# Two-layer diffusion block on one core: input-projection tiles in two pools by chunk parity, attention buffers in pools of their own, halves of the scratch tensors apart, joined stores and outputs, padded addresses

## The chip, the core and the metric

The kernel runs on one core of one Trainium2 chip. The metric is the device time of one execution in microseconds. The core has a matrix engine (TensorE, PE in the profile, whose weight loads are listed as PEld), a vector engine (VectorE, DVE), a scalar engine (ScalarE, ACT), a general engine (GpSimd, POOL) and SyncE (SP), which here only issues DMAs. Data is worked on in SBUF and PSUM and moved to and from DRAM by 16 DMA engines.

## What is computed

The reference is a block of two layers over 2048 latent tokens (a grid of 32 rows by 64 columns) with a prefix of 256 context tokens, all in float32, width 1024:

```
for l in range(DEPTH):                     # 2 layers
    mod, mod_c = silu(c) @ w_mod[l] + b_mod[l], silu(c_ctx) @ w_mod[l] + b_mod[l]
    h, hc = modulate(ln_plain(x), sh1, sc1), modulate(ln_plain(ctx), csh1, csc1)
    qa, ka, va, bx, bb, bc, qn, kn, vn = split(h @ w_in[l])          # and the same of hc
    o_a = windowed_gqa_latent(rope(qa), rope(ka), va, ka_c, va_c, attn_sink[l])
    o_b = gated_short_conv(bx, bb, bc, conv_w[l])
    o_c = neighbourhood_attention_latent(qn, kn, vn, kn_c, vn_c, na_rpb[l])
    mix = concatenate([o_a, o_b, o_c]) @ w_out[l]
    x_mid = ln_affine(DEEPNORM_ALPHA * x + g1 * mix, ln1_g[l], ln1_b[l])
    ...                                    # the context tokens, in layer 0 only
    ffn = expert_choice_ffn(modulate(ln_plain(x_mid), sh2, sc2), w_router[l], w_gate[l], w_up[l], w_down[l])
    x = ln_affine(DEEPNORM_ALPHA * x_mid + g2 * ffn, ln2_g[l], ln2_b[l])
```

Head group A has 6 query heads over 2 key heads, a window of 128 tokens to either side, all context keys and a sink; group C has 6 heads, each query sees 8 grid rows by 16 columns with a bias by relative position, and all context keys.

## The kernel before

A float32 product is made of three matmuls: each operand is split into a high part (ACT's cast) and the low rest (DVE's subtraction), and high x high, low x high and high x low are added in PSUM. Names ending in `h` and `l` are these parts. PE, DVE, ACT, POOL and SP each run their instructions in the order written.

Each layer has four phases. `phase_in` (layer 0: up to about 621 us, layer 1: 2150 to 2714) normalizes the tokens, transposes them into `hh` and `hl`, and multiplies by w_in in five chunks of four 128-token tiles, the last with two. The matmuls are L627 to L629 (columns of C and B) and L805 to L807 (columns of A and V). The parts of queries and keys go to scratch tensors in DRAM: QA and KA for group A, QC and KC for group C. Each is indexed by head, then by part (high or low), then by 64 rows of the head's dimension. SBUF holds two heads over 128 partitions, so each store is cut into two DMAs of 64 partitions (loops over `b` in L659 to L661 and L785 to L788).

`phase_att` (about 621 to 1068, and 2714 to 3120) works through a list of units: A with `u` = 0, 1 (one key head and its three query heads each), and C with `u` = 0 to 5. An A unit has a block for each 128 queries; a C unit has blocks n = 0 to 3 (and n = 4, the context queries, first, in layer 0). A block goes through QK (L1061, L1062), the addition of a mask or bias with the running minimum (L1083, DVE), the exponential (L1091, ACT), transposes (L1108, L1131), copies into `ph` and `pl` (L1220 ACT, L1211 DVE), PV (L1166), a transpose back (L1179), and the division by the sum of the exponentials, which ends in a multiply on DVE (L1191). The result goes to MIXA or MIXC.

Loads are issued by SP in program order. `more_queries` keeps the queries `q` four blocks ahead, `more_values` the values `vw` of C three blocks. The key tile `k` of the next unit (high part on partitions 0 to 63, low on 64 to 127) is loaded by `load_unit`, called in the fifth block of an A unit and the second of a C unit; with it come `vx` and `toep`, from which POOL builds the next unit's bias (L1025) in two buffers, `va` and `bias`. A `k` load reads 128 rows of 2304 numbers, 1152 KB; the first of a layer comes in two parts of 320 and 832 KB, with `maskA` between. DMAs of SP take eight semaphores in turn, so each waits for the one issued eight before it.

`phase_out` multiplies by w_out (L1317) and `phase_moe` runs the 16 experts: gate and up are L1828 to L1830, down is L1865 to L1867.

Of the kernel before, what the change touches and what calls it, by code (L numbers as in the profile page):

```python
# [7 lines left out]
F32 = mybir.dt.float32  # L8
F32R = mybir.dt.float32r
# [3 lines left out]
ALU = mybir.AluOpType  # L13
# [211 lines left out]
def build(ctx, tc, t, out):  # L225
# [4 lines left out]
    const = ctx.enter_context(tc.tile_pool(name="const", bufs=1))  # L230
    dram = ctx.enter_context(tc.tile_pool(name="dram", bufs=1, space=DRAM))
# [10 lines left out]
    half = const.tile([128, 2], F32, name="half")  # L242
# [9 lines left out]
    slotc = const.tile([128, 2], F32, name="slotc")  # L252
# [128 lines left out]
    def mod_piece(l, j, ps, sb, split=True, big="gem", nbig=4, small="tr", apart=False, room=None):  # L381

        pm = ps.tile([128, 512], F32, name=big, bufs=nbig)
# [121 lines left out]
    def phase_in(l):  # L505
        es = ExitStack()
        xp = es.enter_context(tc.tile_pool(name="in_x", bufs=2))
        hp = es.enter_context(tc.tile_pool(name="hT", bufs=2))
        sb = es.enter_context(tc.tile_pool(name="in_sb", bufs=2))
        last = l == DEPTH - 1  # L510

        hT = {-1: [hp.tile([128, KD, 512], F32R, name=z) for z in ("hh", "hl")]}
# [4 lines left out]
        def prep(c):  # L517

            ts = chunk_tiles(c)
            hT[c] = [hp.tile([128, KD, 512], F32R, name=z) for z in ("hh", "hl")]  # L520
# [89 lines left out]
        ps = es.enter_context(tc.tile_pool(name="in_ps", bufs=2, space=PSUM))  # L610
        u = one.tile([128, 2, 516], F32, name="u")
# [3 lines left out]
        def gemm(c):  # L615
# [6 lines left out]
            def s_piece(key, t0=0):  # L622
                wh, wl = W.next(key)
                pg = ps.tile([128, 512], F32, name="gem", bufs=4)
# [7 lines left out]
            def c_rest(f, pg):  # L632
# [106 lines left out]
            def ctx_rest(f, pg):  # L739
# [7 lines left out]
                for a, z in enumerate((sh, sl)):  # L747
                    for b in range(2):
                        SY.dma_start((QA[l][2 * f + b] if f < 3 else KA[l][b])[a, :, 0:256], z.bitcast(F32)[64 * b:64 * b + 64])

            def a_rest(i, pg):
# [32 lines left out]
                for a, o in enumerate((qh, ql)):  # L784
                    for b in range(2):  # L785
                        z = o.bitcast(F32)[64 * b:64 * b + 64]
                        SY.dma_start(QA[l][b::2, a, :, tk].rearrange("f p n -> p f n"), z[:, 0:3, :])
                        SY.dma_start(KA[l][b, a, :, tk], z[:, 3, :])  # L788

            for kind in "AV":  # L790
# [7 lines left out]
                def one_tile(j):  # L798
                    wait_for(c, j)
                    pg = ps.tile([128, 512], F32, name="gem", bufs=4)  # L800
# [9 lines left out]
                def ctx_tiles(f):  # L810
# [3 lines left out]
                    pg = ps.tile([128, 512], F32, name="gem", bufs=4)  # L814
# [45 lines left out]
        if l == 0:  # L860
            for j in range(8):
                next(mod_piece(0, FIRST[j], ps, mb, j % 2 == 1))
                T.tick()
# [13 lines left out]
        for c in range(5):  # L877
            if l == 0 and c == 4:
                T.add(late_constants())
            for what in gemm(c):  # L880
                if what == "mod":
# [3 lines left out]
                    if mods and mods[0][0] == c:  # L885
                        next(mod_piece(0, mods.pop(0)[1], ps, mb))
# [9 lines left out]
    def phase_att(l):  # L896
        es = ExitStack()

        kp = es.enter_context(tc.tile_pool(name="at_k", bufs=2))
        qp = es.enter_context(tc.tile_pool(name="at_q", bufs=1))  # L900
        vwp = es.enter_context(tc.tile_pool(name="at_vw", bufs=3))
        op = es.enter_context(tc.tile_pool(name="at_o", bufs=6))
        mp = es.enter_context(tc.tile_pool(name="at_m", bufs=1))
        vp = es.enter_context(tc.tile_pool(name="at_v", bufs=2))
        sm = es.enter_context(tc.tile_pool(name="at_s", bufs=4))
        pp = es.enter_context(tc.tile_pool(name="at_p", bufs=3))
        hp = es.enter_context(tc.tile_pool(name="at_h", bufs=2))
        wp = es.enter_context(tc.tile_pool(name="at_w", bufs=2))
        bp = es.enter_context(tc.tile_pool(name="at_b", bufs=1))
        psl = es.enter_context(tc.tile_pool(name="at_l", bufs=2, space=PSUM))  # L910
        pst = es.enter_context(tc.tile_pool(name="at_t", bufs=3, space=PSUM))
        pso = es.enter_context(tc.tile_pool(name="at_po", bufs=1, space=PSUM))
# [5 lines left out]
        biases = [None, bp.tile([128, BWID], F32, name="bias")]  # L918
# [11 lines left out]
        NM = len(mem)  # L930
        ulist = [("A", u) for u in range(2)] + [("C", u) for u in range(6)]
# [7 lines left out]
        def load_unit(kind, u):  # L939
            r = units[kind, u] = {}  # L940
            src = (KA if kind == "A" else KC)[l][u].rearrange("a d n -> (a d) n")
            k = r["k"] = kp.tile([128, TT], F32R, name="k")
            vs = VS[l].rearrange("(i p) h d -> p i h d", p=128)
            first = loaded[0] == 0
            if kind == "A":
                r["v"] = v = vp.tile([128, NT, 128], F32R, name="va")
# [9 lines left out]
            if kind == "C":  # L956
                v = vp.tile([128, 2, 128], F32R, name="vx")
# [3 lines left out]
                tz = bp.tile([128, 16, 64], F32, name="toep", bufs=2)  # L961
# [6 lines left out]
        def load_queries(at):  # L968
# [4 lines left out]
            for x, a, y in ((0, 0, 0), (0, 1, 0), (1, 0, 1)):  # L973
                dst = q.bitcast(F32)[64 * a:64 * a + 64, x]
                if kind == "A":
                    SY.dma_start(dst[:, 0:3], QA[l][3 * u:3 * u + 3, y, :, 128 * n:128 * n + 128].rearrange("m d n -> d m n"))
                    continue
# [1006 lines left out]
```

## Time and profile before

| what | before |
|---|---|
| time, median of 3 runs | 4121.46 us (4118.05 to 4125.27) |
| profiled execution, its own time | 4118.59 us |
| its span, first to last instruction | 4116.8 us |
| mean granted TensorE clock | 0.960 of full speed |
| PE busy | 92 % of the span |
| DVE busy | 70 % |
| ACT busy | 49 % |
| POOL busy | 17 % |

The profile is of one execution. Engine shares are means over phases with different limits. SP has no busy share, since issuing a DMA is not counted as work; its timeline shows how long each issue took, with the wait in front of it where it has one. PE's busy time holds the whole length of each matmul, though the next one starts before the last has ended; how fast PE goes is read from the starts. Lines such as L951 are lines of the kernel before.

### The profile page before, as it was taken

Reading aid. Unit: us, or ns where it says so; the run is one execution under the profiler, and the core shown is the slowest. Engines: PE = TensorE matmul, PEld = TensorE weight load, DVE = VectorE, ACT = ScalarE, POOL = GpSimd, SP = SyncE. Lnnn points to the kernel's source line nnn. Section 1 sums busy time; section 2 is a strip of 40 time slices with the busy share of each in tenths; the row PEclk is TensorE's granted clock in tenths of the full one; section 3 lists DMA queues with packets and bytes.
Section 4 is the critical chain, followed back from the end, with each engine's and each line's share of the span. In section 5 each row is a group of like instructions: output and inputs, shape, how many; then the busy total and the mean of one; then the engine's idle time right before and its main releaser. Section 6 shows DMA issues by size and latency. Waiting matters only on the chain. (4 is left out here: it accounts for less than half of the span.)

```text
span 4116.8 us, 64178 instructions
## 1 busy us (share of the span) xinstructions
PE 3801.8 (92%) x22980; PEld 3241.1 (79%) x22980; DVE 2899.2 (70%) x5836; ACT 2007.7 (49%) x3918; POOL 706.6 (17%) x658
## 2 busy tenths in 40 slices
PE   7999999999898899999996999989998966999983
PEld 5877788888787378989985888888897855999972
DVE  6555558999677467767756766469996776777765
ACT  4344337988433044444434434359884332444453
POOL 0000000022123023233311000000221221222214
PEclk9999999999999999999998999999999977999996
DMA  7566665377643677777757766563676424888875
GB/s 227 172 201 206 191 191 143 94 177 175 216 162 122 201 246 219 218 217 216 209 164 225 228 196 188 171 166 107 149 177 225 162 105 153 243 248 255 248 240 184
DMA packets 768951, 785.81 MB, mean 191 GB/s; under 512 B 144912, under 2 KB 650520, under 8 KB 766584
## 3 DMA queue, kind: packets, MB, share of 16 engines
q1 hardware_dynamic: 732776, 657.53, 53.3%
q0 software_dynamic: 34704, 123.13, 10.8%
q8 instruction: 182, 2.98, 0.3%
q14 instruction: 137, 1.12, 0.1%
q10 hardware_dynamic: 1152, 1.05, 0.1%
HBM read 603.05 MB, written 178.48 MB: 190 GB/s over the span
## 5 line engine op out<-in xcount | busy, mean ns | idle before, releaser
L178 ACT CAST wh<-wraw 128x1024 fp32r<-128x1024 f32 x636 | 657.9, 1051 | 387.5 <-DMA wraw<-in_w_in 116.5
L186 DVE TENSOR_TENSOR wl<-wraw,wh 128x1024 fp32r<-128x1024 f32 x636 | 751.2, 1216 | 19.2 <-ACT wh L178 18.8
L1211 DVE TENSOR_TENSOR pl<-pt,ph 128x256 fp32r<-128x256 f32 (+2 forms) x792 | 360.7, 495 | 13.0 <-ACT ph L1220 7.9
L627 PE MATMUL gem<-hh,wh 128*128 128x512 f32 (+1 forms) x960 | 354.5, 369 | 0.0
L628 PE MATMUL gem<-hl,wh 128*128 128x512 f32 (+1 forms) x960 | 352.2, 367 | 0.0
L1091 ACT ACTIVATE p<-lg,mx 128x640 f32<-128x640 f32 (+3 forms) x408 | 332.0, 814 | 37.7 <-DVE mx L1083 36.4
L629 PE MATMUL gem<-hh,wl 128*128 128x512 f32 (+1 forms) x960 | 350.4, 365 | 0.0
L1220 ACT CAST ph<-pt 128x256 fp32r<-128x256 f32 (+2 forms) x792 | 309.5, 446 | 59.1 <-PE pt L1108 53.3
L1828 PE MATMUL pu<-xh,wh 128*128 128x288 f32 (+1 forms) x1024 | 304.6, 297 | 10.1 <-DVE sa L1656 10.1
L1828 PE MATMUL pa<-xh,wh 128*128 128x288 f32 (+1 forms) x1024 | 300.9, 294 | 0.9 <-DVE modc L419 0.9
L1061 PE MATMUL lg<-k,q 128*128 128x384 f32 (+2 forms) x768 | 280.1, 387 | 20.9 <-DMA maskA<-in_maskA 7.4
L1830 PE MATMUL pa<-xh,wl 128*128 128x288 f32 (+1 forms) x1024 | 296.9, 290 | 0.8 <-DVE wl L186 0.8
L1830 PE MATMUL pu<-xh,wl 128*128 128x288 f32 (+1 forms) x1024 | 296.4, 289 | 0.0
L1829 PE MATMUL pa<-xl,wh 128*128 128x288 f32 (+1 forms) x1024 | 294.4, 288 | 0.0
L1829 PE MATMUL pu<-xl,wh 128*128 128x288 f32 (+1 forms) x1024 | 294.1, 287 | 0.0
L1567 POOL DMA_INDIRECT xe<-H,ix x80 | 164.7, 2059 | 473.3 <-DVE ix L1562 398.2
L1062 PE MATMUL lg<-k,q 128*128 128x256 f32 x816 | 228.3, 286 | 0.4 <-ACT p L1091 0.4
L1690 POOL DMA_INDIRECT ACC<-y,ix x62 | 127.1, 2050 | 583.6 <-DVE y L1671 324.3
L1865 PE MATMUL py<-wh,gh 128*128 128x512 f32 x512 | 206.5, 403 | 17.3 <-ACT gh L1658 10.1
L805 PE MATMUL gem<-wh,hh 128*128 128x512 f32 x544 | 220.7, 406 | 0.0
L806 PE MATMUL gem<-wl,hh 128*128 128x512 f32 x544 | 217.3, 399 | 1.4 <-DVE wl L186 1.4
L807 PE MATMUL gem<-wh,hl 128*128 128x512 f32 x544 | 216.9, 399 | 0.0
(346 smaller groups left out, 9681.5 us busy)
## 6 DMA issues: line engine op xcount, KB each, us to landing
wraw<-in_w_in SPq DMA_DIRECT2D x160, 512.0 KB
wraw<-in_w_gate SPq DMA_DIRECT2D x128, 512.0 KB
wraw<-in_w_up SPq DMA_DIRECT2D x128, 512.0 KB
wraw<-in_w_down SPq DMA_DIRECT2D x128, 512.0 KB
wraw<-in_w_mod SPq DMA_DIRECT2D x88, 512.0 KB
vw<-VS SPq DMA_DIRECT2D x192, 128.0 KB
q<-QA SPq DMA_DIRECT2D x204, 96.0 KB
VS<-vs SPq DMA_DIRECT2D x36, 512.0 KB
```

What stands on the lines that cost most here:

```text
L178: self.nc.scalar.copy(h, self.raw[i])
L186: self.nc.vector.tensor_tensor(e[1], self.raw[i], e[0].bitcast(F32), op=ALU.subtract)
L627: P.matmul(pg[:, t0:nt], wh[:, cs_], hh[:, k, t0:nt], start=(k == 0), stop=False)
L628: P.matmul(pg[:, t0:nt], wh[:, cs_], hl[:, k, t0:nt], start=False, stop=False)
L629: P.matmul(pg[:, t0:nt], wl[:, cs_], hh[:, k, t0:nt], start=False, stop=(k == KD - 1))
L1061: P.matmul(pl[:, w0:512], q[:, x, m, :], win(k), start=(x == 0), stop=(x == 1))
L1091: S.activation(p[:, 0:768 - w0], rec["lg"][:, w0:768], AF.Exp, bias=st[b]["mx"][:, m:m + 1], scale=-1.0, accum_out=st[b]["ss"][:, m:m + 1])
L1211: V.tensor_tensor(view(st[b]["pl"]), src, view(st[b]["ph"].bitcast(F32)), op=ALU.subtract)
L1220: S.copy(view(st[b]["ph"]), src)
L1828: P.matmul(pp[f], wh[:, cs_], xh[:, kk, :], start=(kk == 0), stop=False)
L1829: P.matmul(pp[f], wh[:, cs_], xl[:, kk, :], start=False, stop=False)
L1830: P.matmul(pp[f], wl[:, cs_], xh[:, kk, :], start=False, stop=(kk == KD - 1))
```

## The change

- **Scratch layout.** QA, QC and KC change from head, part, row to part, head, row; KA keeps its shape but is indexed by part first. Two heads of one part then lie behind each other, and the two stores of 64 partitions become one of 128. The two parts of one head, which a `k` load reads, now lie apart: the source is taken as two times 64 rows.
- **Pools.** `hh` and `hl` get a pool for odd and one for even chunks, and the projection's PSUM tiles one of their own. Attention's pools are split and put in another order, so that the first `q`, `k`, `maskA` and `va` lie where the last chunk's `hh` and `hl` do not.
- **Joined outputs.** The sums and outputs of up to four A blocks, or two C blocks, are kept together; the small DVE and ACT instructions behind the exponentials and the last multiply run once for such a group. In A units this multiply moves from DVE to POOL, and a group has one MIXA store. The MIXC stores stay as many.
- **Addresses.** `shift` pads and the new pools move where tiles begin in SBUF. The starts of moving and stationary operands of the 512-column matmuls at L627 to L629, L805 to L807, L1317 and L1865 to L1867 all come to lie 32 bytes past a multiple of 64; before, for the stationary ones (L1317, layer 1's L1865 to L1867) or one of the two (the projection), they lay at a multiple of 64. Layer 0's L1865 to L1867 had 32 in both already.

The core of the diff:

```
+    def shift(es, n):
+        pool = es.enter_context(tc.tile_pool(name="shift", bufs=1))
+        pool.tile([128, n // 4], F32, name="shift")
...
-    QA = dr("QA", [6, 2, 64, TT])
+    QA = dr("QA", [2, 6, 64, TT])
     KA = dr("KA", [2, 2, 64, TT])
-    QC = dr("QC", [6, 2, 64, TT])
-    KC = dr("KC", [6, 2, 64, TT])
+    QC = dr("QC", [2, 6, 64, TT])
+    KC = dr("KC", [2, 6, 64, TT])
...
-        hp = es.enter_context(tc.tile_pool(name="hT", bufs=2))
+        hodd = es.enter_context(tc.tile_pool(name="hodd", bufs=1))
+        heven = es.enter_context(tc.tile_pool(name="heven", bufs=1))
...
-                    for b in range(2):
-                        SY.dma_start(dst[2 * (f % 3) + b, a, :, tok + t0:tok + nt],
-                                     z.bitcast(F32)[64 * b:64 * b + 64, t0:nt])
+                    SY.dma_start(dst[a, 2 * (f % 3):2 * (f % 3) + 2, :, tok + t0:tok + nt], z.bitcast(F32)[:, t0:nt])
...
-                    for b in range(2):
-                        z = o.bitcast(F32)[64 * b:64 * b + 64]
-                        SY.dma_start(QA[l][b::2, a, :, tk].rearrange("f p n -> p f n"), z[:, 0:3, :])
-                        SY.dma_start(KA[l][b, a, :, tk], z[:, 3, :])
+                    SY.dma_start(QA[l][a, :, :, tk].rearrange("(f b) p n -> (b p) f n", b=2), o.bitcast(F32)[:, 0:3, :])
+                    SY.dma_start(KA[l][a, :, :, tk], o.bitcast(F32)[:, 3, :])
...
-            src = (KA if kind == "A" else KC)[l][u].rearrange("a d n -> (a d) n")
-            k = r["k"] = kp.tile([128, TT], F32R, name="k")
+            src = (KA if kind == "A" else KC)[l][:, u]
+            k = r["k"] = kp[ulist.index((kind, u)) % 2].tile([128, TT], F32R, name="k")
...
-                SY.dma_start(k.bitcast(F32)[:, 128 * t0:128 * t1], src[:, 128 * t0:128 * t1])
+                SY.dma_start(k.bitcast(F32)[:, 128 * t0:128 * t1], src[:, :, 128 * t0:128 * t1])
...
+            if end:
+                V.reciprocal(of["rs"], of["ss"])
...
-            V.tensor_tensor(o[:, :nm, :], o[:, :nm, :], rec["rs"][:, :nm, None].to_broadcast([128, nm, 64]), op=ALU.mult)
+            (G if kind == "A" else V).tensor_tensor(all_, all_, of["rs"][:, :, None].to_broadcast([128, ng * nm, 64]),
+                                                       op=ALU.mult)
...
+        if last:
+            shift(es, 32)
         sb = es.enter_context(tc.tile_pool(name="moe_sb", bufs=2))
+        shift(es, 96 if last else 32)
```

PE's order does not change. On SP, the first place is the last chunk of layer 0's projection, where the queries and keys of one 128-token tile are stored from `sth` (high) and `stl` (low). Before:

```order
L787 DMA QA_81<-sth 64x3x128
L788 DMA KA_83<-sth 64x128
L787 DMA QA_81<-sth 64x3x128
L788 DMA KA_83<-sth 64x128
L787 DMA QA_81<-stl 64x3x128
L788 DMA KA_83<-stl 64x128
L787 DMA QA_81<-stl 64x3x128
L788 DMA KA_83<-stl 64x128
L736 DMA VS_89<-vs 128x1024
```

And of the change:

```order
L790 DMA QA_80<-sth 128x3x128
L791 DMA KA_82<-sth 128x128
L790 DMA QA_80<-stl 128x3x128
L791 DMA KA_82<-stl 128x128
L742 DMA VS_88<-vs 128x1024
```

Eight stores a tile become four of twice the partitions; the store of VS behind them comes four issues earlier.

The second place on SP is the fourth of the six loads of a C unit's keys in layer 1, with what each row waits for (DMAHW0 to DMAHW7 are the eight semaphores that the DMAs take in turn). Before:

```order
L951 DMA k<-KC_88 128x2304 [waits DMAHW0_49]
L958 DMA vx<-VS_90 128x2x128 [waits DMAHW1_49]
L964 DMA toep<-in_rpb 128x1x1008 [waits DMAHW2_49,Pool_49]
L1199 DMA MIXC_96<-o 8x16x64 [waits DMAHW3_49,DVE_49]
L1199 DMA MIXC_96<-o 8x16x64 [waits DMAHW4_49]
L1199 DMA MIXC_96<-o 8x16x64 [waits DMAHW5_49]
L1199 DMA MIXC_96<-o 8x16x64 [waits DMAHW6_49]
L982 DMA q_27373<-QC_86 64x8x64 [waits DMAHW7_49]
L982 DMA q_27373<-QC_86 64x8x64 [waits DMAHW0_49]
```

And of the change:

```order
L975 DMA k<-KC_87 128x1x2304 [waits DMAHW4_49]
L982 DMA vx<-VS_89 128x2x128 [waits DMAHW5_49]
L988 DMA toep<-in_rpb 128x1x1008 [waits DMAHW6_49,Pool_49]
L1006 DMA q_26886<-QC_85 64x8x64 [waits DMAHW7_49]
L1006 DMA q_26886<-QC_85 64x8x64 [waits DMAHW0_49]
L1006 DMA q_26886<-QC_85 64x8x64 [waits DMAHW1_49]
L1018 DMA vw<-VS_89 32x8x128 [waits DMAHW2_49,PE_49]
L1018 DMA vw<-VS_89 32x8x128 [waits DMAHW3_49]
L1018 DMA vw<-VS_89 32x8x128 [waits DMAHW4_49]
```

The `k` load takes the same place but has another form. The first row behind it that waits for its semaphore is, before, the second `q` (DMAHW0), eight rows on; in the change the third `vw` (DMAHW4), also eight on, since four MIXC stores have moved to where two blocks are stored together.

## Rows read from the trace of the kernel before

**Rows 1.** The page, busy time of each engine (share of the span) xinstructions.

```profile
PE 3801.8 (92%) x22980; PEld 3241.1 (79%) x22980; DVE 2899.2 (70%) x5836; ACT 2007.7 (49%) x3918; POOL 706.6 (17%) x658
```

**Rows 2.** Windows: us, then each engine's busy us (xinstructions), PEclk, DMA share, GB/s.

```profile
640.00:660.00 20.00, 20.00 (x140) 18.53 (x141) 19.61 (x59) 18.43 (x53) 0.00 (x0) 1.00 0.66 177
660.00:730.00 70.00, 69.61 (x492) 63.27 (x491) 69.11 (x222) 64.12 (x196) 0.00 (x0) 1.00 0.38 112
```

**Rows 3.** Windows, columns as above: layer 0's last projection chunk.

```profile
580.00:590.00 10.00, 4.93 (x40) 4.45 (x38) 4.15 (x10) 4.45 (x7) 0.00 (x0) 0.88 0.94 258
590.00:600.00 10.00, 9.59 (x66) 9.62 (x67) 3.23 (x6) 2.07 (x4) 1.12 (x2) 0.78 0.74 205
600.00:620.00 20.00, 20.00 (x169) 20.00 (x168) 11.53 (x24) 5.60 (x10) 0.00 (x0) 1.00 0.52 148
```

**Rows 4.** Timeline of SP in layer 1: start, us, instruction, tile, xcount.

```profile
2992.18 0.45 SPq L951 DMA_DIRECT2D k<-KC  x1
...
2996.87 6.29 SPq L982 DMA_DIRECT2D q<-QC  x3
...
3008.06 1.97 SPq L982 DMA_DIRECT2D q<-QC  x3
...
3025.75 0.46 SPq L951 DMA_DIRECT2D k<-KC  x1
```

**Rows 5.** Timeline of POOL at layer 1's last unit; brackets: idle before, releaser.

```profile
3071.25 3.23 POOL L1025 TENSOR_TENSOR bias<-maskC,toep 128x384 f32<-128x384 f32 x3 [23.89 <-DMA toep<-in_rpb]
```

**Rows 6.** Timeline of DVE at the same place.

```profile
3072.29 0.83 DVE L1083 CUSTOM_DVE_ANT_0 lg<-lg,bias 128x640 f32<-128x640 f32 x1 [0.35 <-POOL bias L1025]
```

**Rows 7.** DMA view, 2837 to 2840.6 us: packets; queue, packets, MB, share of engines.

```profile
DMA packets 448, 1.23 MB, mean 340 GB/s; under 512 B 35, under 2 KB 331, under 8 KB 335
...
q1 hardware_dynamic: 448, 1.23, 89.8%
```

**Rows 8.** DMA view of 3104 to 3112 us: busy tenths of 40 slices.

```profile
DMA  5210341000150000051033034024024005005105
```

**Rows 9.** Timeline of SP in one C unit of layer 0.

```profile
908.52 0.45 SPq L951 DMA_DIRECT2D k<-KC  x1
...
912.95 2.39 SPq L980 DMA_DIRECT2D q<-QC  x3
920.35 1.80 SPq L994 DMA_DIRECT2D vw<-VS  x4
...
946.09 0.45 SPq L951 DMA_DIRECT2D k<-KC  x1
```

**Rows 10.** Timeline of SP from the projection to attention, layer 0.

```profile
611.93 1.19 SPq L660 DMA_DIRECT2D KC<-stl  x2
621.28 1.93 SPq L976 DMA_DIRECT2D q<-QA  x3
...
633.73 0.60 SPq L951 DMA_DIRECT2D k<-KA  x1
```

**Rows 11.** Timelines of PE: layer 0's and layer 1's `down`, the projection.

```profile
1500.56 0.39 PE L1865 MATMUL py<-wh,gh 128*128 128x512 f32 x1
...
1505.59 0.39 PE L1866 MATMUL py<-wl,gh 128*128 128x512 f32 x1
...
3473.42 0.39 PE L1865 MATMUL py<-wh,gh 128*128 128x512 f32 x1
...
3478.81 0.40 PE L1867 MATMUL py<-wh,gl 128*128 128x512 f32 x1
...
134.91 0.39 PE L627 MATMUL gem<-hh,wh 128*128 128x512 f32 x1
...
142.84 0.40 PE L628 MATMUL gem<-hl,wh 128*128 128x512 f32 x1
```

**Rows 12.** Waits, 575 to 600 us: us in total, times, longest.

```profile
DVE stl L650 <- DMA KA<-stl: 6.8, 2, 4.3
```

**Rows 13.** DVE groups by shape, 660 to 730 us: busy us, mean ns.

```profile
L1191 DVE TENSOR_TENSOR o<-o,rs 128x192 f32<-128x192 f32 x14 | 5.0, 355 | 0.0
```

More of the change, by code (lines that the diff above doesn't have):

```diff
@@ L241, in build @@
     G.dma_start(ident, t["ident"])
-    half = const.tile([128, 2], F32, name="half")
+    halves = const.tile([128, 4], F32, name="half")
+    half, slotc = halves[:, 0:2], halves[:, 2:4]
     G.memset(half, -0.5)
@@ L379, in build, with mod_piece @@
     mod_done = set()
-    def mod_piece(l, j, ps, sb, split=True, big="gem", nbig=4, small="tr", apart=False, room=None):
-        pm = ps.tile([128, 512], F32, name=big, bufs=nbig)
+    def mod_piece(l, j, ps, sb, split=True, big="gem", nbig=4, small="tr", apart=False, room=None, acc=None):
+        pm = (acc or ps).tile([128, 512], F32, name=big, bufs=nbig)
         n = 4 if split else 2
@@ L861, in phase_in @@
             for j in range(8):
-                next(mod_piece(0, FIRST[j], ps, mb, j % 2 == 1))
+                next(mod_piece(0, FIRST[j], ps, mb, j % 2 == 1, acc=psg))
                 T.tick()
@@ L885, in phase_in @@
                     if mods and mods[0][0] == c:
-                        next(mod_piece(0, mods.pop(0)[1], ps, mb))
+                        next(mod_piece(0, mods.pop(0)[1], ps, mb, acc=psg))
                     continue
@@ L897, in phase_att, with pool @@
         es = ExitStack()
[L899 to L912, printed above, removed]
+        def pool(name, bufs=1, **kw):
+            return es.enter_context(tc.tile_pool(name=name, bufs=bufs, **kw))
+        qp = pool("at_q")
+        shift(es, 64)
+        kp = [pool("at_k0")]
+        mp = pool("at_m")
+        vp = [pool("at_v0")]
+        pp = pool("at_p", 3)
+        sm = pool("at_s", 3)
+        hp = [pool("at_h0")]
+        lp = [pool("at_w0")]
+        hp.append(pool("at_h1"))
+        lp.append(pool("at_w1"))
+        shift(es, 64)
+        kp.append(pool("at_k1"))
+        vp.append(pool("at_v1"))
+        op = pool("at_o", 3)
+        bsp = pool("at_bias")
+        tp = pool("at_toep", 2)
+        vwp = pool("at_vw", 3)
+        vxp = pool("at_vx", 2)
+        wp = pool("at_ot", 2)
+        bp = pool("at_b")
+        psl = [pool("at_l0", space=PSUM)]
+        pst = pool("at_t", 3, space=PSUM)
+        pso = pool("at_po", space=PSUM)
+        psl.append(pool("at_l1", space=PSUM))
         last = l == DEPTH - 1
@@ L917, in phase_att @@
         maskC = bp.tile([128, 3 * MWID], F32, name="maskC")
-        biases = [None, bp.tile([128, BWID], F32, name="bias")]
+        biases = [None, bsp.tile([128, BWID], F32, name="bias")]
         sink = sinks[:, l, :]
@@ L930, in phase_att @@
         NM = len(mem)
+        group = {}
+        for kind, u in [("A", 0), ("A", 1)] + [("C", u) for u in range(6)]:
+            for rows in (range(2, 6), range(6, 10), range(10, 14), range(14, NT), (0, 1)) if kind == "A" else (
+                    ((4,), (0, 1), (2,), (3,)) if u == 5 else ((4,), (0, 1), (2, 3))):
+                for j, n in enumerate(rows):
+                    group[kind, u, n] = ((kind, u, rows[0]), j, len(rows))
         ulist = [("A", u) for u in range(2)] + [("C", u) for u in range(6)]
@@ L1071, in soft_max @@
             if m == 0:
-                st[b] = {z: sm.tile([128, 4], F32, name=z) for z in ("mx", "ss", "rs")}
+                g, j, ng = group[b]
+                if j == 0:
+                    st["of", g] = {z: sm.tile([128, 12], F32, name=z)[:, 0:ng * nm] for z in ("mx", "ss", "rs")}
+                st[b] = {z: x[:, j * nm:j * nm + nm] for z, x in st["of", g].items()}
             first = 3e38
@@ L1180, in pv @@
             yield
[L1181 to L1184 removed]
+            if j == 0:
+                of["o"] = op.tile([128, 12, 64], F32, name="o")[:, 0:ng * nm, :]
+            all_ = of["o"]
+            o = all_[:, j * nm:j * nm + nm, :]
+            S.copy(o, px[:, :nm, 64:128])
+            if end and kind == "A":
+                V.tensor_tensor(of["ss"], of["ss"], of["rs"], op=ALU.add)
@@ L1192, in pv @@
+            n0 = g[2]
             if kind == "A":
-                SY.dma_start(MIXA[l][128 * n:128 * n + 128, 192 * u:192 * u + 192], o[:, 0:3, :].rearrange("p m d -> p (m d)"))
+                SY.dma_start(MIXA[l][128 * n0:128 * (n0 + ng), 192 * u:192 * u + 192].rearrange("(b p) c -> p b c", p=128),
+                             all_.rearrange("p (b m) d -> p b (m d)", b=ng))
             elif n == 4:
-                SY.dma_start(MIXC[l][0:256, 64 * u:64 * u + 64].rearrange("(m p) d -> p m d", p=128), o[:, 0:2, :])
+                SY.dma_start(MIXC[l][0:256, 64 * u:64 * u + 64].rearrange("(m p) d -> p m d", p=128), all_)
@@ L1196, in pv @@
             else:
                 dst = MIXC[l][256:TT, 64 * u:64 * u + 64].rearrange("(m a g b) d -> m g a b d", m=4, a=8, g=4)
-                for m in range(4):
-                    (G if b == blist[-1] else SY).dma_start(dst[m, n], o[:, m, :])
-            del st[b], blks[b]
+                for x in range(ng):
+                    for m in range(4):
+                        (G if b == blist[-1] else SY).dma_start(dst[m, n0 + x], all_[:, 4 * x + m, :])
+            del st["of", g]
         gens = []
```

57 lines of the change are left out of this document (30 added, 27 removed).

## The prediction

> **What bounds the kernel now.** I read the page first: PE is busy 92 % of the span [rows 1], so most of the kernel is bound by TensorE, and only stretches in which another engine is late, or in which each matmul gets cheaper, can give time. Then the windows, stretch by stretch. The steady A blocks of attention (660 to 730 us) show PE busy 69.61 us and DVE 69.11 us of 70: two engines are full at once, and relieving one hands the bound to the other [rows 2]. The last chunk of the layer-0 projection is the hole in the projection: 40 matmuls in 580 to 590 and 66 in 590 to 600, against 169 in the 20 us from 600 [rows 3]. Last I read SP's queue in the C units, since the change rewrites what SP loads there. In layer 1 one load of `k` comes at 2992.18 and the next at 3025.75, a unit of 33.57 us. In between SP issues almost without a gap, except that three `q` loads that took 1.97 us later took 6.29 us right behind the `k` load: 4.3 us of waiting [rows 4]. So SP, idle by the page's count, is full here. The tables of the next unit are as tight: POOL stood idle 23.89 us until `toep` landed at 3071.25, built its first piece of `bias`, and DVE had already waited 0.35 us for it at 3072.29 [rows 5, 6]. Nothing is to spare in layer 1 between landing and use.
>
> **The change, part by part.**
>
> *The `k` load.* The halves of KA and KC now lie apart in DRAM, so the source of each `k` load is two runs of 64 rows instead of 128 rows in one pattern. What does that cost? In the stretch where a 128-row load (1152 KB, 1.18 MB) makes up nearly all the traffic, the queues moved 340 GB/s with their packets on 89.8 % of 16 engines: 340 / (16 x 0.898) = 23.7 GB/s for each engine, 3.5 us for a load [rows 7]. The MIXC stores are the nearest transfers with a short outer dimension, 8 runs of 16 rows; where only they are under way (3104 to 3112), no slice shows more than 5 tenths of the engines busy [rows 8], against 89.8 % with the 128-row load. Eight outer steps reach about half of the engines. I carry that on: two outer steps reach two of 16. The load then takes 1.18 MB / 47.4 GB/s = 24.9 us. The bounds are these 24.9 us, and 3.5 us if two steps are spread as 128 rows are; I take the first, as the store of 8 steps is nearer to it in form.
>
> The Trainium skill, page "DMA: Bandwidth & Descriptors", section "Why a DMA increments its semaphore by 16 and not by 1", says that a DMA is divided over the largest number of engines, up to 16, that divides the slowest dimension larger than one of both its patterns. That gives 16 engines for the old `k` load, 8 for the MIXC store and 2 for the new load. The trace agrees for the store [rows 8]; no run here shows the two. By this rule the sum is the one below; were it wrong for two, the first rival's.
>
> Who waits: each DMA of SP waits for the one eight before it (the order of the change: `k` on DMAHW4, and the third `vw` behind it, which waits for DMAHW4). Behind it stand the later `vw`, the MIXC stores and the `q` of the next blocks. `toep` is issued two places after `k` and has its own 504 KB over 8 engines: another 64.5 KB / 23.7 = 2.7 us on the two slow engines. With 1 us from issue to start, SP is held until about 28.7 us after the issue of `k`. Before, it was free at 2996.87 + 6.29 = 3003.16, 11.0 us after [rows 4]. So 17 to 18 us are added per load; I take 17.
>
> Layer 1: no slack on SP, so the four intervals between the loads of C1 to C5 grow by 17 each, 68 us; the last load's own lateness falls on C5's first bias, which has no slack [rows 5, 6]: 17 more. 85 in all, 2 less for the slack that the first unit has. Layer 0: its interval is 946.09 - 908.52 = 37.57 us for five blocks. The wait behind `k` and `toep` is the gap from 912.95 + 2.39 = 915.34 to 920.35, and I put the small waits that remain on SP at 3 us [rows 9]. Four intervals grow by 17 - 3 = 14: 56 us. There the load is issued four blocks before its use, 4 x 37.57 / 5 = 30 us, which covers about the first lateness (15 us). 41 us. Sum for C: 83 + 41 = 124, rounded to **+125**. Bounds: 0 (spread) and 10 loads x 17 = 170. The load of C0 and that of A1 lie in the A blocks, whose SP has room; they cost nothing as long as `q` is four blocks ahead.
>
> *Attention's start.* The first `q` load waits no longer for the projection's last matmul: SP issued its last KC store at 611.93 (1.19 us) and the first `q` at 621.28 [rows 10], so loads may start 8 us earlier. But the second part of the first `k` (832 KB, 0.85 MB) takes 0.85 / 47.4 = 18.0 us on two engines: issued at 633.73 - 8, it lands at about 644, where PE was full from 640 on before [rows 2]. **+4 a layer, +8.** Bounds: -8 a layer (spread) and +12 (nothing starts earlier).
>
> *Operand addresses.* The pads and the new pools move where operands begin in SBUF. Layer 0's and layer 1's `down` matmuls (L1865 to L1867) are the same instructions at the same full clock, but in layer 0 both operands begin 32 bytes past a multiple of 64, in layer 1 the stationary one on the multiple. 22 starts in layer 0 take 1505.59 - 1500.56 = 5.03 us, 228.6 ns each; 23 in layer 1 take 3478.81 - 3473.42 = 5.39 us, 234.3 ns. The projection, whose operands differ in this remainder too, takes 142.84 - 134.91 = 7.93 us for 34, 233.2 ns [rows 11]. After the change all of these begin at 32. The compiled program has 2088 (L627 to L629), 1632 (L805 to L807), 1632 (L1317) and 768 (layer 1's `down`) such matmuls of 512 columns, 6120. At 233.2 - 228.6 = 4.6 ns: **-28 us.** Bounds: 0 (layer 1 moves more data at that time, which could be the cause instead) and 5.7 x 6120 = 35.
>
> *Joined stores.* SP's stores of QA, KA, QC and KC halve in number, with the same bytes. In the hole of rows 3, 169 - 40 - 66 = 63 matmuls are missing, 63 x 20/169 = 7.5 us, and DVE there waits up to 4.3 us for a KA store of `stl` [rows 12]. SP reaches that store four issues earlier. I take 5 of the 7.5 us, and the same in layer 1: **-10.** Bounds: 0 (bytes, not issues, are late) and 15.
>
> *Joined outputs.* In A blocks the last multiply (355 ns, 68 times in both layers [rows 13]) goes from DVE to POOL, and three small DVE instructions run once per four blocks. Up to 0.355 x 68 = 24 us of DVE leave, but PE beside it is just as full [rows 2]: **-10**, nearer to the 0 of a PE bound. In C the multiply only changes its shape. POOL's larger multiplies hide in its idle time, a few us once per four blocks; without it the MIXA store would be late, which nobody reads before the output projection. The pools by parity cost nothing in the projection: two tiles before, two after.
>
> Sum against the profiled execution's 4118.59 us: 125 + 8 - 28 - 10 - 10 = +85, 4203.6; the median lies 2.9 above that execution, so **4206 us**.
>
> **The rivals.** (1) *Two outer steps are spread over all engines, or the split costs little*: then the C term is 0 and the start gains 8 a layer: 4121.5 - 28 - 10 - 10 - 16 = 4058, faster. For it: 128 partitions are still written and a row is still 9216 bytes. Against it: rows 8. It decides from a `k` load of about 10 us downward, since 11.0 us after the issue SP is free today. (2) *Two engines, but prefetch covers most of it*: `q` is loaded four blocks ahead and `vw` three, 25 us or more. If each layer loses only about 20 us, 4121.5 + 40 + 8 - 48 = 4122, no change. Against it: the lag adds up over five loads, and in layer 1 `toep` has no slack [rows 5, 6]. (3) *The addresses do nothing*: 28 us more, 4234, with the rest as forecast.
>
> **How the numbers follow.** The forecast with its k load on two engines: 0.60 with the address gain, own range 4165 to 4235; rival 3: 0.16; rival 2, with everything from 4090 to 4150: 0.10; rival 1: 0.14. About 8 us (0.2 %) is what a measurement of this kernel tells from no change. Faster: 0.14 of rival 1 and 0.02 of rival 2; same: 0.04; slower: the rest, 0.80. The range leaves out rival 1 and the top of the C bound: 4100 to 4255.
>
> **What would show it.** Right: SP waits named `DMA k<-KC` of 15 to 20 us in every C unit, C units of about 50 us in both layers, POOL idle on `toep` some 17 us longer, PE far from full in the C windows; `down` matmuls of layer 1 at 229 ns from start to start; more than 106 matmuls in the old hole; A blocks a little shorter. Wrong: a `k` load that lands within 10 us of its issue would undo the largest term and turn the sign; a `vw` wait hidden by prefetch would shrink it.

## The result and the profile after

The changed kernel takes 4358.67 us (median of 4 runs, 4354.17 to 4360.74) against 4121.16 (4118.05 to 4125.27) of the kernel before: ratio 1.0575, 95 % interval 1.056 to 1.059. The forecast was 4206, with 4255 as the upper end. The direction was right and the size far too small, +237 us instead of +85; of the mechanism, the slow `k` load came as forecast, and part of what hangs on it did not.

To see where, I took the start of the same instruction in both traces, from stage to stage (profiled executions, spans 4116.8 and 4356.2 us, both layers together). A C unit is taken to start with DVE's addition (L1083 before) of its first block of latent queries.

| stretch | forecast | measured |
|---|---|---|
| C units, start of unit 0 to start of unit 5 | +125 | 94.2 + 105.4 = +199.6 |
| start of attention, with the second part of the first `k` | +8 | 6.8 + 6.1 = +12.9 |
| A blocks at the loads of A1's and C0's `k` | 0 | 13.1 + 9.5 + 11.5 + 10.3 = +44.4 |
| all the rest | -48 | -17.5 |
| sum | +85 | +239.4 |

The C term lies above its own upper bound of 170.

The page, busy time of each engine, beside [rows 1]:

```profile
PE 3824.4 (88%) x22980; PEld 3278.1 (75%) x22980; DVE 2870.9 (66%) x5574; ACT 2001.6 (46%) x3868; POOL 735.1 (17%) x676
```

PE falls from 92 to 88 % with the same number of matmuls: it waits more.

SP in a C unit of layer 1 answers to [rows 4]:

```profile
3117.45 0.56 SPq L975 DMA_DIRECT2D k<-KC  x1
...
3118.63 4.36 SPq L988 DMA_DIRECT2D toep<-in_rpb  x1
3123.03 20.43 SPq L1006 DMA_DIRECT2D q<-QC  x3
3143.57 4.78 SPq L1018 DMA_DIRECT2D vw<-VS  x4
3148.45 4.94 SPq L1243 DMA_DIRECT2D MIXC<-o  x8
...
3172.14 0.56 SPq L975 DMA_DIRECT2D k<-KC  x1
```

From one `k` to the next it is 54.7 us, 33.57 before. Three `q` loads, right behind `k`, take 20.43 us to issue; SP is through with them at 3143.46, 26.0 us after the `k`. What SP waits for other engines in this unit is 1.6 us in all.

POOL and DVE in the same unit, beside [rows 5, 6]:

```profile
3148.48 3.20 POOL L1049 TENSOR_TENSOR va<-maskC,toep 128x384 f32<-128x384 f32 x3 [43.47 <-DMA toep<-in_rpb]
```

```profile
3149.52 0.83 DVE L1110 CUSTOM_DVE_ANT_0 lg<-lg,va 128x640 f32<-128x640 f32 x1 [19.43 <-POOL va L1049]
```

POOL could start on `toep`, issued behind `k`, 29.9 us after its issue. POOL stood 43.47 us for it (23.89 before, in the last unit), and DVE 19.43 us for POOL (0.35 before). PE waited as well, at the first product of the next unit:

```profile
3144.32 0.66 PE L1085 MATMUL lg<-k,q 128*128 128x384 f32 x1 [14.86 <-issue]
```

The view names no releaser, but this is the first use of the `k` issued at 3117.45. A DMA adds 16 to its semaphore when it lands, in steps, and in the trace the last two steps of this `k` come at 3144.0 and 3144.2, 26.8 us after its issue. So the keys themselves were late, and the table some 4 us more.

The windows (columns as in [rows 2]); first this C unit, then the A blocks:

```profile
3117.40:3172.10 54.70, 38.40 (x269) 34.75 (x268) 33.48 (x79) 31.87 (x78) 9.57 (x9) 0.84 0.49 112
640.00:660.00 20.00, 20.00 (x144) 18.54 (x143) 18.91 (x46) 18.08 (x49) 0.00 (x0) 1.00 0.41 106
660.00:680.00 20.00, 11.71 (x84) 10.61 (x81) 12.74 (x33) 12.32 (x36) 1.47 (x1) 0.85 0.18 63
680.00:700.00 20.00, 17.55 (x107) 16.49 (x108) 13.36 (x35) 12.20 (x34) 0.85 (x1) 0.81 0.61 194
684.00:686.00 2.00, 2.00 (x9) 1.90 (x8) 1.21 (x3) 0.32 (x1) 0.00 (x0) 0.50 0.52 151
688.00:690.00 2.00, 2.00 (x16) 1.82 (x15) 1.41 (x4) 1.10 (x4) 0.00 (x0) 1.00 0.00 0
```

The unit holds 38 us of PE work in 54.7 us. In the A blocks PE, full before, is busy 11.71 us of 20 from 660 on. After the pause it first runs at the lower of its two clock levels (1.2 GHz, a granted clock of 0.50 from 684 to 686), and from 688 on at the higher one again (2.4 GHz, 1.00). With the rest of the pause this leaves 107 matmuls in the 20 us from 680, where 640 to 660 saw 144.

SP and PE's wait at this place:

```profile
649.82 0.52 SPq L975 DMA_DIRECT2D k<-KA  x1
...
653.50 27.02 SPq L1000 DMA_DIRECT2D q<-QA  x6
```

```profile
PE lg L1085 <- DMA q<-QA: 10.7, 1, 10.7
```

Behind A1's `k` six `q` loads take 27.02 us to issue, and PE runs out of queries for 10.7 us. The prediction had put this load at nothing.

In layer 0's C units the picture is another than in layer 1. The waits of SP from 880 to 1120 and of PE from 880 to 1135 hold these lines:

```profile
SPq L1018 <- DMA k<-KC: 21.1, 5, 5.1
```

```profile
PE lg L1086 <- DMA q<-QC: 41.9, 4, 11.6
PE lg L1085 <- DMA q<-QC: 14.6, 4, 4.2
```

After the hold in the issue SP still stands at a `vw` until `k` has landed, five times, each ending 27.0 to 28.7 us after the `k` was issued. PE waits there for queries, 56.5 us in eight waits, and not for the keys. Before that, in unit 0, a store is late, on SP and then on ACT:

```profile
858.72 8.13 SPq L1235 DMA_DIRECT2D MIXA<-o  x1
...
887.52 0.37 ACT L1218 COPY o<-pt 128x256 f32<-128x256 f32 x1 [20.65 <-DMA MIXA<-o]
```

It is the joined store of one group of A's last blocks, the third issue behind C1's `k` (854.17), and its last semaphore step comes at 887.4, behind the `k`'s at 882.9. ACT waits 20.65 us for its buffer of `o` (there are three), and DVE and PE stand behind ACT.

How wide is the `k` load? In 625 to 633 us the second part of layer 0's first `k` is nearly alone under way. The DMA view of that stretch, beside [rows 7, 8]:

```profile
DMA  1010101101011100100110101101011010110101
DMA packets 62, 0.41 MB, mean 52 GB/s; under 512 B 0, under 2 KB 0, under 8 KB 61
...
q1 hardware_dynamic: 61, 0.41, 12.4%
```

12.4 % of 16 engines are 2.0 engines, with 26 GB/s each. That is the forecast's step of two engines (47.4 GB/s). The Trainium skill, page "DMA: Bandwidth & Descriptors", section "Why a DMA increments its semaphore by 16 and not by 1", gives the same two, by its rule of the common divisor; the trace agrees, with 2.0.

The last projection chunk and the first loads, beside [rows 3, 10]:

```profile
580.00:590.00 10.00, 7.53 (x53) 7.29 (x54) 5.30 (x10) 4.05 (x7) 3.03 (x6) 0.83 1.11 359
590.00:600.00 10.00, 10.00 (x87) 10.00 (x87) 5.88 (x8) 4.23 (x7) 0.00 (x0) 1.00 0.67 201
```

```profile
596.65 0.33 SPq L667 DMA_DIRECT2D KC<-stl  x1
597.08 1.98 SPq L1000 DMA_DIRECT2D q<-QA  x3
...
615.50 0.54 SPq L975 DMA_DIRECT2D k<-KA  x1
```

The two slices hold 140 matmuls (106 before), in part because the whole stretch now runs some 6 us earlier. The first `q` now follows the last store at once; before there were 8 us between. From the last projection matmul to the first QK it is 7.2 us (layer 0) and 7.6 us (layer 1) less, as forecast. PE then waits for the second part of `k` until 636.90, 21.4 us after its issue:

```profile
636.90 0.66 PE L1085 MATMUL lg<-k,q 128*128 128x384 f32 x1 [12.38 <-DMA k<-KA]
```

Layer 1's `down`, beside [rows 11]:

```profile
3715.10 0.40 PE L1912 MATMUL py<-wh,gh 128*128 128x512 f32 x1
...
3720.37 0.40 PE L1914 MATMUL py<-wh,gl 128*128 128x512 f32 x1
```

23 starts in 5.27 us are 229.1 ns each (234.3 before), as forecast.

### The profile page after: what moved, and what is told of

It is laid out like the page before. It is cut to its first block, busy times and chain, and to the rows that moved or that the text cites. A ratio compares the mean times of both kernels' runs of the same rounds, so it can differ in the third digit from the quotient of the medians.

```text
span 4356.2 us, 63381 instructions
## 1 busy us (share of the span) xinstructions
PE 3824.4 (88%) x22980; PEld 3278.1 (75%) x22980; DVE 2870.9 (66%) x5574; ACT 2001.6 (46%) x3868; POOL 735.1 (17%) x676
## 5 line engine op out<-in xcount | busy, mean ns | idle before, releaser
L1085 PE MATMUL lg<-k,q 128*128 128x384 f32 (+2 forms) x768 | 291.1, 399 | 192.6 <-issue 97.2
L635 PE MATMUL gem<-hh,wh 128*128 128x512 f32 (+1 forms) x960 | 352.8, 367 | 0.0
L637 PE MATMUL gem<-hh,wl 128*128 128x512 f32 (+1 forms) x960 | 348.4, 363 | 0.0
L1085 PEld LDWEIGHTS lg<-k,q 128*128 128x128 f32 x768 | 152.5, 199 | 212.3 <-issue 167.1
L1912 PE MATMUL py<-wh,gh 128*128 128x512 f32 x512 | 206.1, 402 | 20.9 <-ACT gh L1705 12.5
L808 PE MATMUL gem<-wh,hh 128*128 128x512 f32 x544 | 220.4, 405 | 0.2 <-ACT hh L603 0.2
L1110 DVE CUSTOM_DVE_ANT_0 lg<-lg,maskA,sinks 128x640 f32<-128x640 f32 (+2 forms) x204 | 171.3, 840 | 72.1 <-PE lg L1086 71.8
```

The lines of the kernel that those rows point to most:

```text
L635: P.matmul(pg[:, t0:nt], wh[:, cs_], hh[:, k, t0:nt], start=(k == 0), stop=False)
L637: P.matmul(pg[:, t0:nt], wl[:, cs_], hh[:, k, t0:nt], start=False, stop=(k == KD - 1))
L1085: P.matmul(pl[:, w0:512], q[:, x, m, :], win(k), start=(x == 0), stop=(x == 1))
```

## The experiments

Each kernel is compared with the kernel before on the same chip. Times are medians. e1 to e4 ran on another chip than the rest; the kernel before took 4119.8 us there, and 4123.0 (e5 to e8) and 4121.4 us (e9 to e11) here, so a difference between runs of two such groups is uncertain by some 3 us. Lines of the changed kernel are kept unless the diff shows otherwise.

### Is it the `k` load? (e1, e2, e3, e4)

**e1.** The changed kernel with each `k` load as two DMAs of 64 partitions, each of which reads one run of rows.

```
-                SY.dma_start(k.bitcast(F32)[:, 128 * t0:128 * t1], src[:, :, 128 * t0:128 * t1])
+                for a in range(2):
+                    SY.dma_start(k.bitcast(F32)[64 * a:64 * a + 64, 128 * t0:128 * t1], src[a, :, 128 * t0:128 * t1])
```

> The changed kernel with each k load issued as two DMAs of 64 partitions, one for each half, so that the slowest dimension is 64 again. Theory 1 (the two-run load reaches two DMA engines and all the lost time comes from it): attention's start 7 us earlier in each layer and the cheaper projection, output projection and layer-1 down matmuls stay, the C units go back to about 37 and 33 us, so 4070 to 4095 us. Rival (the joined outputs, POOL's multiply or the new order of the pools cost a good part of the loss): still above 4150 us, with C units above 40 us.

Measured: 4119.16 us, 0.9994 [0.9984, 1.0003]. The whole +237 goes with the two-run form of the `k` load, so that form is its cause. But the 4070 to 4095 were missed: the A blocks and the rest are some 40 us better than before, and the C units lose as much again, 11.8 us in layer 0 and 26.6 in layer 1 (unit 0 to unit 5). SP in one of them:

```profile
3021.16 1.11 SPq L976 DMA_DIRECT2D k<-KC  x2
...
3029.87 7.22 SPq L1019 DMA_DIRECT2D vw<-VS  x4
3037.20 5.19 SPq L1244 DMA_DIRECT2D MIXC<-o  x8
...
3060.77 1.31 SPq L976 DMA_DIRECT2D k<-KC  x2
```

and DVE's waits in layer 1's C units (2945 to 3085 us):

```profile
DVE lg L1111 <- POOL bias L1050: 11.5, 2, 6.6
```

A unit takes 39.6 us where it took 33.6, and DVE waits for the tables. Something besides the slow load is dear in C.

**e2.** The same split for the C units alone; the A units keep the load of two runs.

```
+                if kind == "A":
+                    SY.dma_start(k.bitcast(F32)[:, 128 * t0:128 * t1], src[:, :, 128 * t0:128 * t1])
+                for a in range(2 if kind == "C" else 0):
```

> The changed kernel with the two 64-partition DMAs for the C units' k only; the A units keep the two-run load. Theory 1 splits the loss by the trace into 200 us in the C units and 57 us net in the A units and at attention's start (72 lost, 15 gained): about 4080 + 72 = 4150 us, with the A units as slow as in the changed kernel. Rival (A units are slow because of the joined outputs on POOL): the A units are slow here and in the run with both loads split, and the two runs differ by less than 20 us.

Measured: 4174.32 us, 1.0131 [1.011, 1.0151], 55 above e1. In the trace the first `k` costs 14.7 and 13.6 us more than before, A1's 12.1 and 12.0, and C0's load, split here, nothing. So the loads in the A blocks do cost, 52 us with the first ones. The 4150 were missed by 24 us, as were e1's 4095.

**e3.** The kernel before, with the scratch layout of the change and the load of two runs, nothing else (stores of 64 partitions as before).

```
-    KC = dr("KC", [6, 2, 64, TT])
+    KC = dr("KC", [2, 6, 64, TT])
...
-            src = (KA if kind == "A" else KC)[l][u].rearrange("a d n -> (a d) n")
+            src = (KA if kind == "A" else KC)[l][:, u]
```

> The kernel before with nothing changed but the scratch layout (part, head, row): stores stay at 64 partitions, the k load becomes two runs of 64 rows. Theory 1: the whole loss appears alone, without the gains: 4121 + 200 + 72 = 4390 us, within 30 us. Rival (the two-run load costs what I first worked out, 125 us, and the rest comes from joined outputs and moved MIXC stores): about 4250 us.

Measured: 4381.22 us, 1.0633 [1.0612, 1.0654]. The layout alone gives the loss, 261 us, as expected; all other parts of the change together take back some 23 us. SP of e3:

```profile
3146.80 0.56 SPq L951 DMA_DIRECT2D k<-KC  x1
...
3147.98 3.31 SPq L964 DMA_DIRECT2D toep<-in_rpb  x1
3151.39 19.93 SPq L1199 DMA_DIRECT2D MIXC<-o  x4
...
3200.89 0.56 SPq L951 DMA_DIRECT2D k<-KC  x1
```

Here the four MIXC stores stand behind `k` and `toep`, and they are held 19.93 us (2.50 in a usual block). They don't wait for their data: the multiply that made it (L1191) had ended at 3141.69. The hold falls on whatever is issued next, a store as well as a load.

**e4.** The `k` loads of C units from ACT's queue.

```
-                SY.dma_start(k.bitcast(F32)[:, 128 * t0:128 * t1], src[:, :, 128 * t0:128 * t1])
+                (S if kind == "C" else SY).dma_start(k.bitcast(F32)[:, 128 * t0:128 * t1], src[:, :, 128 * t0:128 * t1])
```

> The changed kernel with the C units' two-run k load issued from ACT's queue instead of SP's. Theory 2 (SP's next DMAs are held in their issue behind the two-run load, so most of the loss in the C units is the queue and not the late keys): the load still takes about 24 us, but SP's q, vw and MIXC go on, toep lands at once, and in layer 1 only the k load's own lateness stays, 24 - 13 = 11 us for each of five units, in layer 0 about none: 4358 - 200 + 55 = 4215 us. Rival (the two slow engines hold everything, whatever queue it is issued from): C units stay at 54 to 57 us and the time at about 4350 us.

Measured: 4409.93 us, 1.0703 [1.0681, 1.0724], slower than the change itself and outside both expectations. ACT reaches the load at 3191.72, 18.4 us after SP's `vx` at 3173.30, and SP stands all the same, in MIXC:

```profile
3182.84 34.26 SPq L1243 DMA_DIRECT2D MIXC<-o  x8
```

SP's waits from 3165 to 3222 tell for what:

```profile
SPq L1243 <- DMA k<-KC: 28.1, 1, 28.1
```

Seven of the stores go out in about 0.6 us each; the eighth waits 28.1 us for the semaphore that ACT's `k` has taken, since the DMAs of both queues take the eight semaphores in turn. SP stands so at all ten loads of C1 to C5, 286.2 us in sum. So the 4215 failed on the wait of the eighth DMA, the one that the prediction had named, and the run doesn't settle what it was made for. Only the load of C0, where SP isn't stopped so early, says something on it: in layer 0 `toep`, issued 1.6 us after ACT's `k`, took 0.68 us to issue (3.76 in the change), but a `q` load 13.1 us after that `k` took 3.21 us (usually 0.6). On another queue the hold is smaller, then, and not gone.

### What paces a C unit (e5, e6, e7, e9)

**e5.** e1, with the outputs of C blocks no longer joined (groups of one block, small pools of their own).

```
-                    ((4,), (0, 1), (2,), (3,)) if u == 5 else ((4,), (0, 1), (2, 3))):
+                    tuple((n,) for n in (4, 0, 1, 2, 3))):
```

> The kernel with the k load as two 64-partition DMAs, and the C blocks' outputs no longer joined (every C block has its own multiply and its four MIXC stores, as before the change; A stays joined). In the run with two loads the C units still lose 11 us in layer 0 and 24 us in layer 1 against the kernel before. Theory (the four MIXC stores that used to stand right behind the unit's load covered part of SP's wait for it; joined, they stand in one row of eight elsewhere): the C units return to the kernel before within 5 us a layer, 4085 to 4095 us. Rival (two 64-partition loads are themselves slower than one of 128): C units stay as in the run with two loads, about 4115 us.

Measured: 4095.72 us, 0.9938 [0.9922, 0.9955], 23 below e1. Layer 0's C units are back at their length of before (11.8 us lost in e1, -1.0 here), as expected; layer 1's still lose 14.5, which the theory didn't have.

**e6.** The changed kernel with `vx` and `toep` issued ahead of `k`, so that the table isn't behind the slow load.

> The changed kernel, two-run k load kept, with vx and toep issued ahead of the C units' k instead of behind it. Theory (SP is held in the issue of what follows the k load, so SP's own cycle of about 55 us a unit sets the pace): toep lands early, but the C units keep 52 to 57 us, 4335 to 4360 us. Rival (the pace is set by toep, which lands after k and lets POOL start the bias some 17 us late): the layer-1 units lose only k's own lateness of 11 to 13 us instead of 21, 4290 to 4310 us.

Measured: 4365.67 us, 1.0589 [1.0567, 1.061]. SP:

```profile
3129.65 0.54 SPq L987 DMA_DIRECT2D k<-KC  x1
3130.23 24.68 SPq L1007 DMA_DIRECT2D q<-QC  x3
...
3185.07 0.53 SPq L987 DMA_DIRECT2D k<-KC  x1
```

The table is no longer late, and the unit is as long (55.4 us, though the time is 6 us above the theory's range): the `q` loads take over `toep`'s share of the hold. So the table doesn't set the length of a C unit. SP's issue does, as far as the traces show: in the change's unit SP waits 1.6 of 54.7 us for other engines. Downstream of it PE now waits for the keys alone, at five units of layer 1 (3100 to 3330):

```profile
PE lg L1086 <- DMA k<-KC: 99.7, 5, 20.6
```

How much of this would stay if nothing behind `k` were held, no run shows.

**e7.** The change, with the keys in their old layout and one `k` load of 128 rows; the stores of Q stay joined, those of K are two again; C outputs apart as in e5.

```
-    KC = dr("KC", [2, 6, 64, TT])
+    KC = dr("KC", [6, 2, 64, TT])
...
-            src = (KA if kind == "A" else KC)[l][:, u]
+            src = (KA if kind == "A" else KC)[l][u].rearrange("a d n -> (a d) n")
```

> The changed kernel with the keys stored as before the change (head, part, row, two stores of 64 partitions; k is one load of 128 rows), queries stored joined in the new layout, C outputs not joined. Theory: as the run with two loads and C apart, and one DMA issue less per unit: 4075 to 4090 us, 30 to 45 us below the kernel before. Rival (the joined key stores bring part of the projection's gain): 5 to 10 us slower than that run.

Measured: 4083.32 us, 0.9908 [0.9891, 0.9924], as expected, and faster than both kernels. Its windows and DVE's wait in layer 1's C units:

```profile
2956.70:2990.80 34.10, 34.10 (x255) 30.84 (x254) 32.62 (x80) 30.08 (x74) 9.83 (x9) 1.00 0.80 178
```

```profile
DVE lg L1120 <- POOL bias L1058: 1.7, 1, 1.7
```

PE is full again, at full clock. Against e5 the time still lost in layer 1 is gone (14.5 us there, 1.0 here): two 64-partition loads in the place of one were the rest of e1's loss.

**e9.** e7 with the C outputs joined again.

> The kernel with the old key layout (k one load of 128 rows), with the C blocks' outputs joined in pairs again. Theory (joining takes the four MIXC stores away from behind the unit's load and costs about 12 us a layer, whatever form the load has): 4083 + 24 = 4107 us. Rival (joined stores cost only where the k load is cut in two and SP has one DMA more): 4083 to 4088 us.

Measured: 4090.27 us, 0.9919 [0.9901, 0.9936], 7 above e7, between the two expectations. In the trace the stretch from unit 1 to unit 5 is 12 us longer than in e7 in layer 1, and 1.6 in layer 0. SP and DVE there:

```profile
2961.70 0.45 SPq L982 DMA_DIRECT2D k<-KC  x1
...
2967.38 7.67 SPq L1025 DMA_DIRECT2D vw<-VS  x4
2975.62 4.95 SPq L1251 DMA_DIRECT2D MIXC<-o  x8
...
2999.40 0.45 SPq L982 DMA_DIRECT2D k<-KC  x1
```

```profile
DVE lg L1118 <- POOL bias L1056: 8.7, 2, 5.7
```

The unit is 37.7 us instead of 34.1. With MIXC's eight stores at once the order behind `k` is another, and the tables come later. So joined C outputs cost 7 us (the four times of each kernel don't overlap, the two intervals do), and some 23 where the `k` load is two DMAs.

### The small terms (e8, e10, e11)

**e8.** e1 without the `shift` pads and with two constants apart again, which puts the operands back to the start addresses of before.

```
-        shift(es, 64)
...
-        if last:
-            shift(es, 32)
-        shift(es, 96 if last else 32)
```

> The kernel with the k load as two 64-partition DMAs, without the pads and with the constants apart again, so that all matmul operands begin at the same remainders of 64 bytes as in the kernel before. Theory (operand starts cost 4 to 5 ns a matmul where the two differ): the starts go back to 233 to 234 ns and the time rises by what the trace shows gained, about 18 us, to 4137 us. Rival (the address does nothing): 4119 us as with the pads, within 4 us.

Measured: 4129.42 us, 1.0011 [1.0001, 1.0021], 10 above e1 (7, if each is taken against the kernel before on its chip) and between the two expectations. The mean starts in layer 1's `down` go back to 234.1 ns (229.2 in the change) and in layer 0's projection at L635 to L637 to 233.5 (229.2). In the stretches with these matmuls the trace gives 5.1 + 4.8 in layer 0's projection and output projection, 5.2 + 1.9 + 2.1 in layer 1's with the experts: 19 us. Half of it comes back in the C units, 9.7 us shorter than in e1, which are not bound by PE there; why exactly, this run doesn't tell.

**e10.** e7 with the Q stores cut into 64 partitions again.

> The same kernel with C apart and old key layout, and the stores of the queries cut into 64 partitions again: all scratch stores as before the change. My term for joined stores was 10 us for both layers; the traces so far show the last chunk only 1 to 3 us shorter than operand addresses alone explain. Theory now (bytes and not issues are late in that hole): 4083 to 4087 us. Rival (the 10 us of the prediction): 4090 us or more, though half of it might be the key stores, which are apart in both.

Measured: 4085.83 us, 0.9915 [0.9897, 0.9933], 2.5 above e7 and not resolved from it, as the theory had it.

**e11.** e7 with the outputs of A blocks apart and their multiply on DVE.

> The same kernel with C apart and old key layout, and with A's outputs undone as well: the multiply on DVE, small DVE and ACT instructions and a MIXA store for each A block, as before the change. The prediction gave joined A outputs 10 us; the traces show A blocks 0.07 us shorter, 68 of them, and about 1.4 us at each change of units. Theory: 4083 + 5 to 8 = 4088 to 4091 us. Rival (A is bound by PE, joining gives nothing): 4083 us.

Measured: 4084.69 us, 0.991 [0.9892, 0.9927], 1.4 above e7, not resolved, and below the 4088 to 4091 of the theory. In the trace, from the first QK to C unit 0, e7 is 2.8 us (layer 0) and 0.9 us (layer 1) shorter.

## Why the prediction was right in direction and wrong in size

**Right.** Two outer steps reach two engines (52 GB/s, 2.0 engines). The layout alone makes the loss (e3), the form of the load alone takes it away (e1). The start of attention, +8 forecast, is +12.9: 7.2 and 7.6 us earlier, and 14.1 and 13.7 us lost on the second part of the first `k`. Rivals 1 and 2 fall by the same rows, rival 3 by the 229.1 ns and by e8. Of the signs named, POOL's longer wait for `toep` came (43.47 against 23.89 us), the SP waits named `DMA k<-KC` of 15 to 20 us in every C unit did not: 5.1 us at most in layer 0's C units, none in layer 1's.

**Failed: "SP is held until about 28.7 us after the issue of `k`" by the wait of the eighth DMA, so "17 to 18 us are added per load".** The moment was about right, the way to it and what follows were not. In layer 0 the eighth DMA did stand for `k`, until 27.0 to 28.7 us after the issue. In layer 1 SP was let go at 26.0 us and never stood there. In both it had before that been held in the issue of the DMAs right behind `k` (in layer 1 `toep` 4.36 us instead of 0.66, three `q` 20.43 instead of 1.97). In the 11.0 us of before it had also issued four MIXC stores; now none. What was left to issue took 54.7 - 26.0 = 28.7 us, against 33.57 - 11.0 = 22.6: the MIXC stores all stand behind it (4.94 twice, before 2.5 three times), and `vw` takes 4.78 and 3.10 instead of some 2 each. So this unit grew by 15.0 + 6.1 = 21.1 us, where the forecast had 17; the five grew by 17.3 to 23.5, 105.4 in layer 1, forecast 83. The larger miss is layer 0, 94.2 instead of 41. There I let the four blocks of lead cover the first lateness and spread 56 us over four intervals. The lead covers the keys, but PE waited for the queries issued behind them (56.5 us from 880 on), and all five units grew (20.9 us in unit 0, which was the MIXA store, 73.3 in the four behind it). The C term was short by 75 us.

**Failed: the loads of C0 and A1 "cost nothing as long as `q` is four blocks ahead".** It isn't at that place. When SP comes to the `q` behind `k`, three blocks are loaded: 3 x 5.67 us (the distance of two MIXA stores before, 706.50 and 712.16) = 17 us. The hold is 27.02 less the 3.8 us that six `q` usually take (two took 1.27 just ahead of it), 23.2 us, and then the queries have still to land (PE goes on at 682.45, 4.2 us after the third was issued): PE's wait of 10.7 us is what stays bare. PE then loses some 2.4 us more at the lower clock (9 matmuls in 2 us against 16, for some 5 us). The four loads cost 9.5 to 13.1 us each, 44.4 in all. e2 brings A1's part back alone.

**Failed: "In C the multiply only changes its shape."** The joining also puts eight MIXC stores in a place on SP where there were four: 7 us (e9; 13.7 by the trace of its C units), some 23 with two `k` DMAs (e5 against e1). In the change it is part of the 199.6.

**Failed: a late MIXA store is one "which nobody reads before the output projection".** Nobody reads it, but its buffer is written again: ACT's 20.65 us in unit 0 of layer 0. e3, which has the slow load and no joined outputs, grows by 8.4 us in that unit and by 174.5 in the C term, the change by 20.9 and 199.6. By this comparison, in which the other parts of the change stand too, some 25 us of the C term go with the joined outputs; no run takes them alone away from the slow load.

**Mis-sized.** Operand addresses, -28: 19 us in their own stretches (e8), since the matmuls at L808 to L810 hardly changed (234.2 to 233.3 ns) and layer 0's `down` became slower (229.4 to 231.0). Joined stores, -10: e8, which keeps them, has the layer-0 projection 2.2 us shorter (0.9 of it at the very start) and layer 1's not at all, and e10 finds 2.5 us, not resolved, for those of Q. Joined outputs of A, -10: 3.7 us by e11's trace, and 1.4 by its time, not resolved.

**Open.** Why the issue behind a two-engine load is held (e3 and e6 show that it hits whatever comes next, e4 doesn't separate queue and engines); what a C unit would lose by the late keys alone; why L808 to L810 keep their 233 ns with both operands at 32; what the C units gain in e8.

## What to carry to other kernels

Before two stores are joined by changing a layout in DRAM, look at the outer dimension that the loads get: here the two runs turned a load of all engines into one of two, and lost some 240 to 260 us (e1 against the change, e3) for stores that were worth about 2 us, not resolved. Price a slow DMA not only by its own lateness, but by everything that is issued right behind it and by the stock that its consumers hold at that very block. Where a queue is as full as a unit is long, any regrouping of its DMAs is a change of the path.

## What the runs showed of the hardware

DMAs behind a load on two engines are slow already in their issue: 4.36 us for `toep` (0.66), 20.43 for three `q` (1.97), 19.93 for four MIXC stores (2.50). They also land late: `vx`, issued 0.6 us behind the `k` of 3117.45, had 14 of its 16 semaphore steps by 3121.3 and the last two at 3144.4 and 3144.5, right after the last two of `k`.

The 512-column matmuls of the projection (L635 to L637) and of layer 1's `down` start 4 to 5 ns later, each, where one operand begins at a multiple of 64 bytes than where both begin 32 past it (233.5 against 229.2 ns, 234.1 against 229.2); e8 turns this back by moving addresses alone. L808 to L810 don't follow it (233.3 ns with both at 32), so the condition isn't complete.
